# The last 128 tokens leave a dense expert product, and are summed from gathered rows

## The chip, the cores and the metric

The kernel runs on one core of a Trainium2 chip. The metric is the device time of one execution in microseconds (us); the time before is the median of three runs. The profile is of one further execution.

Engines are named as the profile names them: PE is TensorE (matmuls; PEld its weight loads), DVE is VectorE, ACT is ScalarE, POOL is GpSimd and SP is SyncE, which here only issues DMAs.

## What is computed

Two transformer blocks run one after the other on 512 tokens of width 1024, all in float32. The change touches only the last layer of the second block, an expert layer (PEER) with 128 x 128 = 16384 experts. An expert is one row of `u` and one row of `v`. Each token has 8 heads, and each head picks 16 experts, so a token sums 128 rows of `v`:

```python
def peer(hn, w_q, subkeys, u, v):
    q = (xt @ w_q).reshape(T, H, 2, PEER_QDIM // 2)
    s = jnp.einsum('thcd,cnd->thcn', q, subkeys)
    s1, i1 = lax.top_k(s[:, :, 0], K)             # K = 16, H = 8
    s2, i2 = lax.top_k(s[:, :, 1], K)
    cand = (s1[..., :, None] + s2[..., None, :]).reshape(T, H, K * K)
    sc, ci = lax.top_k(cand, K)
    idx = e1 * PEER_NKEYS + e2                    # e1, e2: entries of i1, i2 that ci names
    g = jax.nn.softmax(sc, axis=-1)
    a = jnp.einsum('cd,chkd->chk', xc, u[ic])     # ic: idx of these tokens
    act = gelu(a) * gc                            # gc: g of these tokens
    return jnp.einsum('chk,chkd->cd', act, v[ic])
```

## The kernel before

Activations lie transposed, feature on the partition and the 512 tokens along the free axis. The expert layer (`peer`) does not gather. It computes all 16384 activations of every token densely, multiplies them by a matrix G that is zero where a token did not pick the expert, and multiplies the result by all of `v`.

**Exact float32 by two halves.** A float32 operand is split into a high part in the faster format float32r and a low part, the rest. `mm3` (L317 to L322) makes a product of three matmuls: high by high, low by high, high by low. The weights are split on the way (`split`, L271): ACT copies the high part (`wh`), DVE subtracts (`wl`). `lin2` (L1096) loads one 512 KB weight tile (`raw`) with a DMA on SP, splits it and runs 8 x 3 matmuls of 512 columns into one PSUM bank (`acc1`). Three raw tiles and three split tiles are held.

**Routing** (`route`, `weights`, L1647 to L1740). For each block of 128 tokens DVE finds the 16 best of each key half and of the candidates, and leaves the experts' two numbers e1, e2 and the gates g, transposed by PE. `weights` builds G in DRAM, 16 tokens at a time: one-hot tiles on DVE and ACT, four matmuls of 256 columns for four tokens (L1734), and a store of 1 MB by POOL. There are 32 such time blocks, 512 matmuls.

**First product** (`up`, L1762). Unit e multiplies `u` by the activations, 24 matmuls, and applies gelu on ACT; SP stores the result GA[e] in DRAM. 128 units are needed. They are given out between the steps of routing by a running account of DVE's and ACT's estimated work (`PEER_NS`, `ROUTE_NS`), so that PE has matmuls while routing runs. 121 are done in that way, seven more in the first group of the second product.

**Second product** (L1781 to L1801). 16 groups of 8 units. POOL loads the group's slice of G (`gt`, 2 MB) and each unit's GA (`ga`, 256 KB); DVE multiplies them, ACT copies the high part and DVE subtracts (`hid`, 18 tiles: two for each of 8 units and one pair more). Then eight output tiles d follow, each a `lin2` over `v` with 24 matmuls of 512 columns, and DVE adds the bank into the residual X[d]. 16 x 8 x 24 = 3072 matmuls.

The tile framework sets the order of each engine's instructions from the written code and puts in the waits; an engine runs its own list in order.

A second form of matmul occurs early: `mod_group` (L467) multiplies a 128 x 32 float32 weight, and four such matmuls write to four groups of 32 output partitions:

```python
for k in range(8):
    j = 32 * (k % 4)
    nc.tensor.matmul(p[j:j + 32, 0:256], self.cs[:, k, :], ws[k], start=k < 4, stop=k >= 4, tile_position=(0, j))
```

Of the kernel before, what the change touches and what calls it, by code (L numbers as in the profile page):

```python
# [13 lines left out]
D, S, SC, T = 1024, 512, 256, 768  # L14
# [25 lines left out]
NGA = 6  # L40
# [31 lines left out]
TBW = 16  # L72
NTB = S // TBW
# [5 lines left out]
SHARE = 3  # L79
# [103 lines left out]
def pack2(i, o):  # L183
# [34 lines left out]
    o["pv"] = i["peer_v_2"].reshape(128, 16, 8, 8, 128).transpose(1, 3, 0, 2, 4)  # L218
    c, s = rope2_tables(np.arange(S))
# [11 lines left out]
    iota = np.tile(np.arange(128), (128, 1))  # L231
# [12 lines left out]
class K:  # L244
# [1357 lines left out]
    def peer(self, hs):  # L1602
# [14 lines left out]
        rt = fr.enter_context(self.tc.tile_pool(name="rt", bufs=1))  # L1617
        SCO = {}
# [13 lines left out]
        ET = [rt.tile([128, S], F32, name=n) for n in ("e1T", "e2T", "gT")]  # L1632
        GT = [rt.tile([128, S], F32R, name=n) for n in ("ghT", "glT")]
        U32 = mybir.dt.uint32
        CNT = [16 // (i + 1) for i in range(16)]
# [11 lines left out]
        def route(b):  # L1647
# [56 lines left out]
            p = self.acc1()  # L1704
            for j, src in enumerate((e12[:, 0], e12[:, 1], gz.rearrange("p h k -> p (h k)"))):
                nc.tensor.transpose(p[:, j * 128:j * 128 + 128], src, self.eye)
                nc.scalar.copy(ET[j][:, b * 128:b * 128 + 128], p[:, j * 128:j * 128 + 128])
            cs = slice(b * 128, b * 128 + 128)
            nc.scalar.copy(GT[0][:, cs], ET[2][:, cs])
            nc.vector.tensor_tensor(GT[1][:, cs], ET[2][:, cs], GT[0][:, cs], op=OP.subtract)  # L1710
# [31 lines left out]
        def routing():  # L1742

            for ns in route(0):
                yield ns, 0
            for b in range(4):
                r = route(b + 1) if b < 3 else iter(())
                due = 0.0
                for tb in range(NTB // 4 * b, NTB // 4 * (b + 1)):
                    for ns in weights(tb, SHARE if b == 3 else 0):  # L1750
                        yield ns
                        due += ROUTE_NS
                        while due > 0:
                            ns = next(r, None)
                            if ns is None:
                                break
                            due -= ns
                            yield ns, 0
                for ns in r:
                    yield ns, 0  # L1760

        def up(e, ahead):  # L1762
# [3 lines left out]
            if ahead:  # L1766
                GA[e] = dp.tile([128, S], F32, name=f"GA{e}")
                nc.sync.dma_start(out=GA[e], in_=ga)
            return ga

        GA = {}
        todo = [8 * g + e for g in list(range(2, 16, 2)) + list(range(1, 16, 2)) + [0] for e in range(8)]
        due = [0.0, 0.0]
        for ns in routing():
            due = [x + y for x, y in zip(due, ns)]
            while max(due) > PEER_NS and todo:
                due = [max(x - PEER_NS, 0.0) for x in due]
                up(todo.pop(0), True)
        fr.close()
        rb = self.es.enter_context(self.tc.tile_pool(name="rb", bufs=1))  # L1780
        for g in range(16):  # L1781
            gt = self.t("gt", [128, NTB, 8, TBW], bufs=2, pool=rb)
            nc.gpsimd.dma_start(out=gt.rearrange("p b e t -> p b (e t)"),
                                in_=G[:, :, 8 * g:8 * g + 8, :].rearrange("b p e t -> p b (e t)"))
            hid = []
            for e in range(8):
                if 8 * g + e in GA:
                    ga = self.t("ga", [128, S], bufs=NGA, pool=rg)
                    nc.gpsimd.dma_start(out=ga, in_=GA[8 * g + e])
                else:  # L1790
                    ga = up(8 * g + e, False)
                gv = ga.rearrange("p (b t) -> p b t", t=TBW)
                nc.vector.tensor_tensor(gv, gv, gt[:, :, e, :], op=OP.mult)
                hi = self.t("hid", [128, S], F32R, 18, rb)
                lo = self.t("hid", [128, S], F32R, 18, rb)
# [76 lines left out]
```

## Time and profile before

| what | value |
|---|---|
| median of 3 runs | 3765.06 us (3758.55 to 3765.51) |
| the profiled execution | 3763.02 us |
| its span, first to last instruction | 3761.3 us |
| granted TensorE clock, mean | 0.989 |
| PE busy | 3657.0 us, 97% |
| DVE / ACT / POOL busy | 2461.8 / 1749.6 / 159.2 us |
| moved by DMA | 490.28 MB |
| routing with units of the first product | 2360 to 3021 us |
| second product | 3060.5 to 3757.6 us |

The three runs lie within 0.2% of each other. A matmul's shown duration is its latency; matmuls overlap in the pipeline, and the distance between two starts is what one costs in a row. A line like L322 is that of a helper that serves the whole kernel, so the tile names tell which product a matmul belongs to: `hs` is the first product's input, `hid` the second's. A matmul of two float32 operands that are not float32r appears as two records.

### The profile page before, as it was taken

Reading aid. Unit: us, or ns where it says so; the run is one execution under the profiler, and the core shown is the slowest. Engines: PE = TensorE matmul, PEld = TensorE weight load, DVE = VectorE, ACT = ScalarE, POOL = GpSimd, SP = SyncE. Lnnn points to the kernel's source line nnn. Section 1 sums busy time; section 2 is a strip of 40 time slices with the busy share of each in tenths; the row PEclk is TensorE's granted clock in tenths of the full one; section 3 lists DMA queues with packets and bytes.
Section 4 is the critical chain, followed back from the end, with each engine's and each line's share of the span. In section 5 each row is a group of like instructions: output and inputs, shape, how many; then the busy total and the mean of one; then the engine's idle time right before and its main releaser. Section 6 shows DMA issues by size and latency. Waiting matters only on the chain.

```text
span 3761.3 us, 52800 instructions
## 1 busy us (share of the span) xinstructions
PE 3657.0 (97%) x19762; PEld 3004.0 (80%) x19762; DVE 2461.8 (65%) x4950; ACT 1749.6 (47%) x3452; POOL 159.2 (4%) x317
## 2 busy tenths in 40 slices
PE   8998999999999999999999999999999999999999
PEld 5866788888877878887778877878888888888887
DVE  5976644444788755564777669998766855555554
ACT  5267531111446732233566543777877733322232
POOL 0000000000000000000001000000000011111110
PEclk9999999999999999999999999999999999999999
DMA  6430432221341233334432333455555566666553
GB/s 210 132 107 13 123 118 63 67 63 62 106 144 56 74 118 95 95 96 137 117 98 83 100 98 115 155 171 177 184 179 171 199 212 200 201 196 192 189 185 115
DMA packets 155248, 490.28 MB, mean 130 GB/s; under 512 B 18368, under 2 KB 24832, under 8 KB 150768
## 3 DMA queue, kind: packets, MB, share of 16 engines
q1 hardware_dynamic: 128368, 374.48, 31.4%
q0 software_dynamic: 26624, 112.43, 8.8%
q8 instruction: 156, 2.56, 0.3%
q14 instruction: 100, 0.82, 0.1%
HBM read 408.86 MB, written 74.71 MB: 129 GB/s over the span
## 4 chain that ended last, share of the span: by engine, by line
PE 86%; DVE 8%; ACT 3%; DMA 2%; issue 1%; SPq 0%; ACTq 0%; POOL 0%; DVEq 0%; POOLq 0%
PE b L322 57%; PE a L322 19%; PE b L467 1%; DVE wl L277 1%; PE a L1734 1%; PE b L917 1%; PE b L568 1%; PE b L906 1%; PE b L1365 1%; PE a L1125 0%; DMA mraw<-in_wmod_dram 0%; DVE gst L1738 0%; PE b L1174 0%; ACT P L896 0%; DMA mg<-in_wmod_dram 0%
## 5 line engine op out<-in xcount | busy, mean ns | idle before, releaser
L276 ACT CAST wh<-raw 128x1024 fp32r<-128x1024 f32 (+2 forms) x531 | 547.3, 1031 | 1363.2 <-PE b L322 810.2
L322 PE MATMUL b<-hs,wh 128*128 128x512 f32 x2624 | 822.4, 394 | 4.4 <-ACT hs L1092 4.4
L277 DVE TENSOR_TENSOR wl<-raw,wh 128x1024 fp32r<-128x1024 f32 (+2 forms) x531 | 635.2, 1197 | 169.7 <-ACT wh L276 157.7
L322 PE MATMUL b<-hid,wh 128*128 128x512 f32 x2048 | 630.9, 389 | 0.0
L322 PEld LDWEIGHTS b<-hs,wh 128*128 128x128 f32 x2624 | 487.1, 190 | 107.3 <-ACT hs L1092 5.3
L322 PE MATMUL b<-hs,wl 128*128 128x512 f32 x1312 | 516.1, 393 | 0.9 <-DVE wl L277 0.9
L322 PEld LDWEIGHTS b<-hid,wh 128*128 128x128 f32 x2048 | 384.4, 188 | 80.6 <-DVE hid L1797 0.6
L322 PE MATMUL b<-hid,wl 128*128 128x512 f32 x1024 | 398.4, 389 | 0.0
L322 PE MATMUL b<-hh,wh 128*128 128x256 f32 (+1 forms) x1160 | 364.5, 351 | 3.7 <-DVE V L840 2.2
L322 PE MATMUL a<-hh,wh 128*128 128x512 f32 (+1 forms) x1144 | 354.6, 348 | 9.5 <-DVE y L1046 7.2
L322 PE MATMUL b<-hl,wh 128*128 128x256 f32 (+1 forms) x1160 | 356.0, 343 | 0.3 <-DVE hl L534 0.3
L322 PE MATMUL b<-hh,wl 128*128 128x256 f32 (+1 forms) x1160 | 355.0, 343 | 0.0
L322 PE MATMUL a<-hh,wl 128*128 128x512 f32 (+1 forms) x1144 | 349.8, 344 | 1.5 <-DVE wl L277 1.5
L322 PE MATMUL a<-hl,wh 128*128 128x512 f32 (+1 forms) x1144 | 350.5, 344 | 0.3 <-DVE hl L534 0.3
L322 PEld LDWEIGHTS b<-hs,wl 128*128 128x128 f32 x1312 | 248.2, 189 | 53.4 <-DVE wl L277 1.3
L322 PEld LDWEIGHTS b<-hh,wh 128*128 128x128 f32 x1160 | 200.3, 188 | 44.1 <-issue 4.8
L322 PEld LDWEIGHTS a<-hh,wh 128*128 128x128 f32 x1144 | 197.0, 188 | 44.6 <-issue 13.9
L322 PEld LDWEIGHTS b<-hl,wh 128*128 128x128 f32 x1160 | 200.7, 189 | 30.1 <-issue 1.2
L322 PEld LDWEIGHTS b<-hid,wl 128*128 128x128 f32 x1024 | 192.2, 188 | 39.6
L322 PEld LDWEIGHTS b<-hh,wl 128*128 128x128 f32 x1160 | 200.0, 188 | 27.9 <-issue 1.1
L322 PEld LDWEIGHTS a<-hl,wh 128*128 128x128 f32 x1144 | 197.2, 188 | 31.1 <-issue 2.9
L322 PEld LDWEIGHTS a<-hh,wl 128*128 128x128 f32 x1144 | 196.9, 188 | 30.6 <-DVE wl L277 2.3
(412 smaller groups left out, 5323.1 us busy)
## 6 DMA issues: line engine op xcount, KB each, us to landing
raw<-in_w_dram SPq DMA_DIRECT2D x134, 512.0 KB
raw<-in_pu_dram SPq DMA_DIRECT2D x128, 512.0 KB
raw<-in_pv_dram SPq DMA_DIRECT2D x128, 512.0 KB
raw<-in_win_dram SPq DMA_DIRECT2D x64, 512.0 KB
G<-gst POOLq DMA_DIRECT2D x32, 1024.0 KB, 4.9
gt<-G POOLq DMA_DIRECT2D x16, 2048.0 KB, 14.1
mraw<-in_wmod_dram SPq DMA_DIRECT2D x82, 384.0 KB
GA<-ga SPq DMA_DIRECT2D x121, 256.0 KB
```

The source lines that it names most:

```text
L276: nc.scalar.copy(hi, raw)
L277: nc.vector.tensor_tensor(lo, raw, hi, op=OP.subtract)
L322: nc.tensor.matmul(o, w[wi], xx[xi], start=start and xi == 0 and wi == 0, stop=stop and wi == 1)
L467: nc.tensor.matmul(p[j:j + 32, 0:256], self.cs[:, k, :], ws[k], start=k < 4, stop=k >= 4, tile_position=(0, j))
L568: nc.tensor.matmul(p[:, :w], self.ones[1024], s, start=k == 0, stop=k == 7)
L906: nc.tensor.transpose(p[:, j * 128:j * 128 + 128], Ps[e][:, kc * 128:kc * 128 + 128], self.eye)
L917: nc.tensor.matmul(o[pr, c % 2 * 128:c % 2 * 128 + 128], V[i][:, kc, pr], PT[e * nkb + kc], start=kc == 0, stop=kc == nkb - 1, tile_positi ...
L1365: nc.tensor.transpose(p[:, j * 128:j * 128 + 128], src, self.eye)
L1734: nc.tensor.matmul(p[:, i * 256:i * 256 + 256], A[:, i], W[:, i].rearrange("p j e -> p (j e)"), start=True, stop=True)
```

## The change

The first 384 tokens (`SG`) stay in the dense way; G has 24 time blocks of 16 tokens instead of 32, and the second product's matmuls have 384 columns. For the last 128 tokens:

- `route(3)` does not fill the tables for `weights`. It leaves two tiles of row numbers, `IV` (row of `v` of each pick and token, picks on the partition) and `IG` (place of the pick's activation in a DRAM array `GU`), and the gates `G3`.
- `up` stores the last 128 columns of each unit in `GU`; all 128 units now run before the second product, and none in it.
- Token t = 32 j + m belongs to column group j. For each m of 32, `rows(m)` fetches for four tokens their 128 rows of `v` (512 KB a token, by indirect DMA on POOL), `acts(m)` fetches their 128 activations (4 bytes each), multiplies them by the gates and puts them in column m of a 128 x 32 tile that is else zero (`az`). `sums(m)` runs eight fp32 matmuls into two banks `po`, that are held over all 32 sums.
- After the last unit, ACT copies `po` out, PE transposes it in eight pieces and DVE adds these to X.
- gt and ga loads move from POOL's queue to SP's; `ga` for the second product gets its own tiles `gd` (eight) in the pool `rb`, which takes the memory of the two pools given up after the first product.

```diff
-NTB = S // TBW
+SG = 384
+NTB = SG // TBW
+NVR = 8
...
-    def lin2(self, ap, hs, shape=(128, 8, 128)):
+    def lin2(self, ap, hs, shape=(128, 8, 128), n=S):
         w = self.wunit(ap, shape)
-        p = self.acc1()
+        p = self.acc1()[:, :n]
...
+            if last:
+                nc.vector.scalar_tensor_tensor(IV, dst[0], 128.0, dst[1], op0=OP.mult, op1=OP.add)
+                nc.vector.scalar_tensor_tensor(dst[0], dst[1], 128.0, dst[0], op0=OP.mult, op1=OP.add)
+                nc.vector.scalar_tensor_tensor(IG, dst[0], 128.0, iota, op0=OP.mult, op1=OP.add)
...
-        def up(e, ahead):
+        def up(e):
             p = self.lin2(a["pu"][e], hs)
-            ga = self.t("ga", [128, S], bufs=NGA, pool=rg)
+            ga = self.t("ga", [128, S], bufs=NGA, pool=ru)
             nc.scalar.activation(ga, p, AF.Gelu_apprx_tanh)
...
+            GA[e] = dp.tile([128, SG], F32, name=f"GA{e}")
+            nc.sync.dma_start(out=GA[e], in_=ga[:, :SG])
+            nc.sync.dma_start(out=GU[e], in_=ga[:, SG:])
...
+        for e in todo:
+            up(e)
         fr.close()
...
+        def rows(m):
+
+            for j in range(4):
+                v = VR[m, j] = self.t("vr", [128, D], bufs=NVR, pool=rb)
+                t = 32 * j + m
+                nc.gpsimd.indirect_dma_start(out=v, out_offset=None, in_=a["vn"],
+                                             in_offset=bass.IndirectOffsetOnAxis(ap=IV[:, t:t + 1], axis=0))
+
+        def acts(m):
+
+            c = self.t("ac", [128, 4], bufs=4, pool=rb)
+            for j in range(4):
+                t = 32 * j + m
+                nc.gpsimd.indirect_dma_start(out=c[:, j:j + 1], out_offset=None, in_=GU.rearrange("e p (t o) -> (e p t) o", o=1),
+                                             in_offset=bass.IndirectOffsetOnAxis(ap=IG[:, t:t + 1], axis=0))
+            nc.vector.tensor_tensor(c, c, G3[:, m::32], op=OP.mult)
+            z = VR[m] = self.t("az", [128, 4, 32], bufs=3, pool=rb)
+            nc.vector.tensor_tensor(z, c[:, :, None].to_broadcast([128, 4, 32]), hot[:, None, 31 - m:63 - m].to_broadcast([128, 4, 32]), op=OP.mult)
+
+        def sums(m):
+            z = VR.pop(m)
+            v = [VR.pop((m, j)) for j in range(4)]
+            for h in range(0, D, 512):
+                for j in range(4):
+                    nc.tensor.matmul(po[32 * j:32 * j + 32, h:h + 512], z[:, j, :], v[j][:, h:h + 512],
+                                     start=m == 0, stop=m == 31, tile_position=(0, 32 * j))
...
+            if g < 15:
+                load_gt(g + 1)
             for d in range(8):
-                p = self.lin2(a["pv"][g, d], hid)
-                nc.vector.tensor_tensor(X[d], X[d], p, op=OP.add)
+                if g < 15:
+                    load_ga(8 * g + 8 + d)
+                p = self.lin2(a["pv"][g, d], hid, n=SG)
+                nc.vector.tensor_tensor(X[d][:, :SG], X[d][:, :SG], p, op=OP.add)
+                m, r = divmod(8 * g + d, 4)
+                if r == 1 and m < 31:
+                    acts(m + 1)
+                if r == 2:
+                    sums(m)
+                    if m < 30:
+                        rows(m + 2)
+        y = self.t("vr", [128, D], bufs=NVR, pool=rb)
+        nc.scalar.copy(y, po)
```

On PE, between two units of the second product, before; a unit's 24 matmuls end and the next unit's begin at once (`b` is the accumulator, `hid` the split activations, `wh` and `wl` the split weights):

```order
L322 MATMUL b_29053<-hid_28973,wl_29050 128x512
L322 MATMUL b_29053<-hid_29011,wh_29049 128x512
L322 MATMUL b_29053<-hid_29012,wh_29049 128x512
L322 MATMUL b_29053<-hid_29011,wl_29050 128x512
L322 MATMUL b_29085<-hid_28745,wh_29081 128x512
L322 MATMUL b_29085<-hid_28746,wh_29081 128x512
```

The same place now, after the third unit of the first group:

```order
L325 MATMUL b_28614<-hid_28524,wh_28610 128x384
L325 MATMUL b_28614<-hid_28525,wh_28610 128x384
L325 MATMUL b_28614<-hid_28524,wl_28611 128x384
L1823 MATMUL a_28479<-vr_28463,az_28486 32x512
L1823 MATMUL a_28479<-vr_28465,az_28486 32x512
L1823 MATMUL a_28479<-vr_28467,az_28486 32x512
L1823 MATMUL a_28479<-vr_28469,az_28486 32x512
L1823 MATMUL a_28479<-vr_28463,az_28486 32x512
L1823 MATMUL a_28479<-vr_28465,az_28486 32x512
L1823 MATMUL a_28479<-vr_28467,az_28486 32x512
L1823 MATMUL a_28479<-vr_28469,az_28486 32x512
L325 MATMUL b_28664<-hid_28489,wh_28660 128x384
```

Eight matmuls of the sums stand between units, once in four units, and a unit's matmuls are narrower.

On POOL, at the end of routing before: the loads for the second product follow the last store of G directly, while PE's list has the 168 matmuls of seven units between the last routing matmul and the first on `hid`:

```order
L1740 DMA G<-gst_28407 128x2048
L1789 DMA ga_28742<-GA_28704 128x512
L1740 DMA G<-gst_28586 128x2048
L1783 DMA gt_28740<-G 128x32x128
L1783 DMA gt_29271<-G 128x32x128
L1789 DMA ga_29273<-GA_24465 128x512
```

The same loads now, on SP, at the end of the first product:

```order
L1782 DMA GA_28398<-ga_28396 128x384
L1783 DMA GU<-ga_28396 128x128
L285 DMA raw_28692<-in_pv_dram 128x1024
L1782 DMA GA_28434<-ga_28432 128x384
L1783 DMA GU<-ga_28432 128x128
L285 DMA raw_28726<-in_pv_dram 128x1024
L1828 DMA gt_28445<-G 128x24x128
L1833 DMA gd_28447<-GA_20741 128x384
```

The loads of gt and gd moved behind the two stores of the last unit of the first product; weight tiles for the first six units of the second product stand ahead of them. PE's list has 600 matmuls, 25 units, between the last routing matmul and the first on `hid`.

On POOL in the middle of the second product before, the loads of one group:

```order
L1783 DMA gt_30213<-G 128x32x128
L1789 DMA ga_29936<-GA_25303 128x512
L1789 DMA ga_29943<-GA_25359 128x512
L1789 DMA ga_29950<-GA_25423 128x512
L1789 DMA ga_30215<-GA_21234 128x512
```

And now, the gathers for one sum, of activations (`ac`) and of rows (`vr`):

```order
L1812 DMA ac_29844<-GU,ig 128x1 x4
L1804 DMA vr_29010<-in_vn_dram,iv 128x1024
L1804 DMA vr_29012<-in_vn_dram,iv 128x1024
L1804 DMA vr_29014<-in_vn_dram,iv 128x1024
L1804 DMA vr_29016<-in_vn_dram,iv 128x1024
```

POOL has eight indirect DMAs for each sum in place of nine plain ones for each group of eight units.

## Rows read from the trace of the kernel before

**Rows 1.** The page: busy times and the chain that ended last

```profile
PE 3657.0 (97%) x19762; PEld 3004.0 (80%) x19762; DVE 2461.8 (65%) x4950; ACT 1749.6 (47%) x3452; POOL 159.2 (4%) x317
...
PE 86%; DVE 8%; ACT 3%; DMA 2%; issue 1%; SPq 0%; ACTq 0%; POOL 0%; DVEq 0%; POOLq 0%
PE b L322 57%; PE a L322 19%; PE b L467 1%; DVE wl L277 1%; PE a L1734 1%; PE b L917 1%; PE b L568 1%; PE b L906 1%; PE b L1365 1%; PE a L1125 0%; DMA mraw<-in_wmod_dram 0%; DVE gst L1738 0%; PE b L1174 0%; ACT P L896 0%; DMA mg<-in_wmod_dram 0%
```

**Rows 2.** Stretches: us; busy PE, PEld, DVE, ACT, POOL; clock; DMA share; GB/s

```profile
2360.00:3021.00 661.00, 655.90 (x3100) 546.65 (x3099) 533.69 (x1147) 505.01 (x1274) 16.55 (x31) 1.00 0.53 179
3021.00:3060.50 39.50, 38.62 (x173) 31.68 (x172) 18.48 (x22) 15.05 (x23) 6.69 (x8) 1.00 0.81 252
3060.50:3757.60 697.10, 697.02 (x3074) 576.38 (x3072) 380.09 (x497) 203.41 (x249) 86.27 (x130) 1.00 0.58 182
3757.60:3761.30 3.70, 0.00 (x0) 0.00 (x0) 0.65 (x1) 0.00 (x0) 0.00 (x0) 0.93 0.19 71
```

**Rows 3.** Groups of PE in the second product: busy us, mean ns, idle before

```profile
L322 PE MATMUL b<-hid,wh 128*128 128x512 f32 x2048 | 630.9, 389 | 0.0
L322 PE MATMUL b<-hid,wl 128*128 128x512 f32 x1024 | 398.4, 389 | 0.0
```

**Rows 4.** Timeline of PE, 384-column matmuls: start us, us, instruction

```profile
2051.67 0.33 PE L322 MATMUL a<-hi,qhi 128*128 128x384 f32 x1
...
2053.41 0.33 PE L322 MATMUL a<-hi,qlo 128*128 128x384 f32 x1
```

**Rows 5.** Groups of DVE in the second product

```profile
L1793 DVE TENSOR_TENSOR ga<-ga,gt 128x512 f32<-128x512 f32 x121 | 79.0, 685 | 105.9 <-DMA ga<-GA 105.9
L1797 DVE TENSOR_TENSOR hid<-ga,hid 128x512 fp32r<-128x512 f32 x122 | 77.3, 684 | 1.4 <-ACT hid L1796 1.4
```

**Rows 6.** Routing's matmuls: their group, and the timeline at the first

```profile
L1734 PE MATMUL a<-ohW,ohA 128*128 128x256 f32 x512 | 80.8, 287 | 10.5 <-ACT ohW L1730 10.2 <-DVE gst L1738 0.3
...
2351.08 1.46 PE L1734 MATMUL a<-ohW,ohA 128*128 128x256 f32 x4 [5.42 <-ACT ohW L1730]
```

**Rows 7.** fp32 matmuls: timelines of mod_group and of L1174, and their groups

```profile
100.13 1.07 PE L467 MATMUL b<-mraw,cs 128*32 128x256 f32 x16
101.13 0.50 PE L322 MATMUL a<-hh,wh 128*128 128x512 f32 x1
...
L467 PE MATMUL b<-mraw,cs 128*32 128x256 f32 x656 | 55.1, 393 | 3.0 <-DMA mraw<-in_wmod_dram 3.0
...
1798.15 1.02 PE L1174 MATMUL b<-sq,c 128*128 128x512 f32 x2
...
L1174 PE MATMUL b<-sq,c 128*128 128x512 f32 x36 | 18.6, 598 | 0.0
```

**Rows 8.** Groups of ACT from 2360 to 3060 us: gelu, and the high part

```profile
L1765 ACT ACTIVATE ga<-b 128x512 f32<-128x512 f32 x114 | 67.2, 590 | 0.3 <-PE b L322 0.3
L1796 ACT CAST hid<-ga 128x512 fp32r<-128x512 f32 x7 | 4.3, 622 | 12.8 <-issue 6.7 <-DVE ga L1793 6.1
```

**Rows 9.** SP's issues of the outputs: duration ns min/median/max, first and last

```profile
L1852 SPq DMA_DIRECT2D out_dram<-x x8: 332/338/344, 3720.2 to 3758.3; - x8
```

**Rows 10.** From issue to landing: all DMAs of GA, and gt's loads

```profile
DMA to landing us min/median/max: 3.0/4.9/14.5
...
gt<-G POOLq DMA_DIRECT2D x14, 2048.0 KB, 14.1
```

**Rows 11.** Stretches, as in rows 2: after routing's first wait, and the fullest DMA

```profile
2347.70:2354.40 6.70, 3.32 (x9) 2.89 (x10) 6.70 (x23) 4.94 (x16) 0.00 (x0) 0.50 0.36 117
...
20.00:30.00 10.00, 7.72 (x63) 2.63 (x62) 7.55 (x17) 6.32 (x11) 0.00 (x0) 0.83 1.03 407
```

**Rows 12.** Groups of POOL in the second product

```profile
L1789 POOL DMA_DIRECT2D ga<-GA x116 | 62.5, 539 | 542.3 <-DVE hid L1797 535.9 <-issue 2.4
L1783 POOL DMA_DIRECT2D gt<-G x14 | 23.8, 1703 | 24.9 <-DVE ga L1793 24.9
```

**Rows 13.** DMA queue of POOL in the second product: packets, MB, share of 16 engines

```profile
q0 software_dynamic: 16694, 59.83, 26.9%
```

More of the change, by code (lines that the diff above doesn't have):

```diff
@@ L218, in pack2 @@
     o["pv"] = i["peer_v_2"].reshape(128, 16, 8, 8, 128).transpose(1, 3, 0, 2, 4)
+    o["vn"] = i["peer_v_2"]
     c, s = rope2_tables(np.arange(S))
@@ L1704, in route @@
             p = self.acc1()
+            last = b * 128 >= SG
+            dst = [self.t("e3", [128, 128], bufs=2, pool=rt) for _ in range(2)] + [G3] if last else [e[:, b * 128:b * 128 + 128] for e in ET]
             for j, src in enumerate((e12[:, 0], e12[:, 1], gz.rearrange("p h k -> p (h k)"))):
                 nc.tensor.transpose(p[:, j * 128:j * 128 + 128], src, self.eye)
[L1707 to L1710, printed above, removed]
+                nc.scalar.copy(dst[j], p[:, j * 128:j * 128 + 128])
+            if last:
+                nc.vector.scalar_tensor_tensor(IV, dst[0], 128.0, dst[1], op0=OP.mult, op1=OP.add)
+                nc.vector.scalar_tensor_tensor(dst[0], dst[1], 128.0, dst[0], op0=OP.mult, op1=OP.add)
+                nc.vector.scalar_tensor_tensor(IG, dst[0], 128.0, iota, op0=OP.mult, op1=OP.add)
+            else:
+                cs = slice(b * 128, b * 128 + 128)
+                nc.scalar.copy(GT[0][:, cs], ET[2][:, cs])
+                nc.vector.tensor_tensor(GT[1][:, cs], ET[2][:, cs], GT[0][:, cs], op=OP.subtract)
             yield 0
@@ L1745, in routing @@
                 yield ns, 0
-            for b in range(4):
-                r = route(b + 1) if b < 3 else iter(())
+            for b in range(3):
+                r = route(b + 1)
                 due = 0.0
-                for tb in range(NTB // 4 * b, NTB // 4 * (b + 1)):
-                    for ns in weights(tb, SHARE if b == 3 else 0):
+                for tb in range(NTB // 3 * b, NTB // 3 * (b + 1)):
+                    for ns in weights(tb, SHARE if b == 2 else 0):
                         yield ns
@@ L1760, in routing @@
                     yield ns, 0
-        def up(e, ahead):
+        def up(e):
             p = self.lin2(a["pu"][e], hs)
-            ga = self.t("ga", [128, S], bufs=NGA, pool=rg)
+            ga = self.t("ga", [128, S], bufs=NGA, pool=ru)
             nc.scalar.activation(ga, p, AF.Gelu_apprx_tanh)
[L1766 to L1769, printed above, removed]
+            GA[e] = dp.tile([128, SG], F32, name=f"GA{e}")
+            nc.sync.dma_start(out=GA[e], in_=ga[:, :SG])
+            nc.sync.dma_start(out=GU[e], in_=ga[:, SG:])
         GA = {}
-        todo = [8 * g + e for g in list(range(2, 16, 2)) + list(range(1, 16, 2)) + [0] for e in range(8)]
+        todo = list(range(128))
         due = [0.0, 0.0]
@@ L1781, in peer, with load_ga @@
+        def load_ga(e):
+            gas[e] = self.t("gd", [128, SG], bufs=8, pool=rb)
+            nc.sync.dma_start(out=gas[e], in_=GA[e])
+        hot = rb.tile([128, 64], F32, name="hot")
+        nc.gpsimd.memset(hot, 0.0)
+        nc.gpsimd.memset(hot[:, 31:32], 1.0)
+        load_gt(0)
+        for e in range(8):
+            load_ga(e)
+        for m in range(2):
+            rows(m)
+        po = self.acc()
+        acts(0)
         for g in range(16):
-            gt = self.t("gt", [128, NTB, 8, TBW], bufs=2, pool=rb)
@@ L1783, in peer @@
-            nc.gpsimd.dma_start(out=gt.rearrange("p b e t -> p b (e t)"),
-                                in_=G[:, :, 8 * g:8 * g + 8, :].rearrange("b p e t -> p b (e t)"))
+            gt = gts.pop(g)
             hid = []
             for e in range(8):
[L1787 to L1791, printed above, removed]
+                ga = gas.pop(8 * g + e)
```

27 lines of the change are left out of this document (22 added, 5 removed).

## The prediction

> **What bounds the kernel now.** I read the busy times first, then the chain of waits, then a table of stretches, then the groups of instructions of the last stretch, and only after that the queues. TensorE is busy for 97% of the span, and the chain that ended last lies on it for 86%, 57% in matmuls into the one-bank accumulators [rows 1]. The table of stretches says where: from 2360 us on PE never rests, and the stretch from 3060.5 to 3757.6 us, the second product of the experts, is 697.1 us with 697.02 us of PE busy [rows 2]. In it stand 3072 matmuls of 512 columns (2048 + 1024) with no idle time before them [rows 3]. So one costs 697.1 / 3072 = 0.227 us; its shown mean of 0.389 us is latency. Other engines have room there: DVE 380 us, ACT 203 us, POOL 86 us, and the DMA engines are at 0.58 at 182 GB/s [rows 2]. Time comes off the span where PE gets less to do, as long as nothing with room now runs out of it.
>
> **The dense product.** It keeps its 3072 matmuls but each has 384 columns. The trace has eleven such matmuls back to back, from 2051.67 to 2053.41 us: ten steps of 0.174 us [rows 4]. 3072 x 0.174 = 534.5 us, so **-162.6 us**. DVE's and ACT's share of that work shrinks with it: their 512-wide groups [rows 5] become 384 wide.
>
> **The routing weights.** A quarter of the 512 matmuls on L1734 goes, 128. A quarter of their 80.8 us [rows 6] is 20, but that counts tails that lie over the next matmul; at half a 512-column matmul's 0.227 it is 15. I take **-16 us**. The DVE and ACT work that goes with them lay under PE and gives nothing more. The first wait of this stage, 5.42 us for ACT [rows 6], comes before any of the removed blocks and stays.
>
> **The new sums.** 32 times eight fp32 matmuls of 512 columns, each using 32 columns of the array, in four column groups. mod_group has the same form with 256 columns: its eight matmuls are 16 records and take 1.00 us from the first start to the next instruction's [rows 7]; one record lasts 0.393 us on average, so one after the other without overlap they would take over 3 us. Four run at once: four sets at (1.07 - 0.39) / 3 = 0.22 us. Of the two records of a 512-column fp32 matmul the second starts 1.02 - 0.60 = 0.42 us after the first (L1174: the pair's extent less one duration) [rows 7]; with the rounding I take 0.43, so 0.86 for a whole one. So one sum is 4 x 0.43 = 1.72 us, and changing the array's form costs what the 1.00 us has over 4 x 0.22, some 0.12 us, and about as much on the way in. 32 x 1.95 = **+62 us**; bounds 55 (no change of form) and 220 (no overlap: 256 x 0.86).
> The Trainium skill (TensorEngine Tiling, Key Properties) says that a change of tiling mode drains the array; the trace agrees, with the 0.12 us. Its page TensorE: Matmul & The Clock Gate (Measured speedup vs the span model) gives 2.38x for three column tiles; four at that efficiency would be 3.2x, and the sums would be an estimated 75 us instead of 62. The rows above show nearer to four, so I stay at 62.
>
> **The stage boundary.** Before, the first G tile is read by POOL as soon as routing ends, and seven expert units of the first product still run on PE meanwhile; PE is busy 38.62 of 39.5 us there [rows 2]. Now all 128 units come first and 25 of them follow the last routing matmul, but the first gt load stands on SP's queue behind the stores of the last unit, and its buffers are those of a pool that must be given up, so it waits for these stores too. Nothing on PE covers this chain: gelu 0.59 [rows 8]; two store issues at 0.33 [rows 9] and a landing of at least 3.0 us (median 4.9, which includes reads), I take 3.5 [rows 10]; the gt load, 14.1 us for 2 MB [rows 10], three quarters of which is 10.6, lengthened because eight row gathers of 512 KB start with it, so 13 (at most double, 21); the first gd behind it, 1; multiply and cast at three quarters of 0.685 and 0.62 [rows 5, 8], 1. That is 20 us. Then the first unit goes at DVE's pace: eight experts at two operations of 0.51 us are 8.2 us against PE's 4.2, so 4 more. After an idle 5.42 us the granted clock was 0.50 for 6.7 us, the 1.2 GHz level [rows 6, 11]; most of that falls into DVE's pace, 1 more. **+25 us**, bounds 16 and 38.
>
> **The end.** Now only the last of the eight outputs is late: from the last matmul to the end 3.7 us [rows 2]. After, all eight wait for the 128-column additions, behind a copy (which a last dense unit hides) and eight transposes: about 1 us of PE, then eight issues at 0.338 us [rows 9] and 2.1 MB to write at 314 to 395 GB/s (below), 5.3 to 6.7 us. **+7 us** in all, bounds 3 and 10.
>
> **Queues, and what hides.** POOL loses ga and gt loads (0.54 and 1.70 us each [rows 12]) and gets 256 indirect DMAs. No row shows an indirect one. With those two as bounds they are 138 to 436 us of POOL in a stage of 534.5 + 62 = 596, so hidden; they bind from 596 / 256 = 2.3 us each. A sum's rows are asked for two sums (37 us) ahead, and a POOL wait there holds up only later gathers. SP gets gt and gd loads between its weight loads, so a late gd holds up raw tiles behind it, and DVE, which already waits 105.9 us for ga [rows 5], waits for gd in front of wl. Three weight tiles split ahead are 12.5 us of cover instead of 16.3.
> The DMA engines: weights 67.1 MB, rows 67.1, gd 25.2, gt 25.2, together 184.6 MB. At the stage's own rate per share, 182 / 0.58 = 314 GB/s, that is 588 us; at the fullest stretch of the trace, 407 GB/s at 1.03 [rows 11], so 395, it is 467 us. Added to this are 16384 gathered single elements, 1024 an engine. Their price is between nothing and a whole packet's: q0's 16694 packets took 26.9% of 16 engines over 697 us [rows 13], 0.18 us, so 0 to 184 us in all. I take 0.06 us, 61 us, since four bytes move but a packet has a fixed part; this is the softest number here. Sum: 528 to 649 us against PE's 596 + 25. So DMA nearly fills the stage without setting its length, and bursts will cost PE something: **+12 us**, bounds 0 and 50.
>
> **Sum.** -162.6 - 16 + 62 + 25 + 7 + 12 = -72.6. The profiled execution took 3763.0 us (span 3761.3), so 3690.4; the median of the runs is 2.0 higher, so the forecast is **3692 us**.
>
> **Rivals.** (a) *The DMA engines set the stage.* For it: 588 + 61 = 649 us above. Against: 407 GB/s was reached. The stage takes 649 + 25 instead of 596 + 12 + 25: 3733 us. From 0.09 us an element (681 - 588 = 93 us over 1024) the whole gain is gone. The Trainium skill (DMA: Bandwidth & Descriptors, Specifications) says that a transfer under 512 B makes the engine read, modify and write, which speaks against these element gathers; it states no price, and no run here shows one. (b) *POOL sets the stage, slower than before.* If one indirect DMA takes POOL 3 us, 256 are 768 us: 768 - 596 - 12 = +160, 3852 us. It turns slower from (608 + 73) / 256 = 2.66 us. For it: the indices must be read from SBUF and 128 addresses built. Against: 4096 pieces of 512 B took only 1.70 us [rows 12]. (c) *The column groups don't run at once* with 512 columns and four different right-hand tiles: 220 us for 62, 3850 us. Against: the four at once in [rows 7]. (d) *Almost no bubble and no stalls:* bubble 16, bursts 0, end 3: 3692 - 9 - 12 - 4 = 3667 us, with shorter sums (55) 3660.
>
> **How the numbers follow.** Forecast 0.62 (own range 3670 to 3720), (d) 0.09, (a) 0.18, (b) 0.08, (c) 0.03. A difference of 0.2%, 7.5 us, is about what a measurement tells from no change. Of (a) I give 0.11 to faster, 0.04 to within, 0.03 to slower. Faster: 0.62 + 0.09 + 0.11 = 0.82; same 0.04; slower 0.03 + 0.08 + 0.03 = 0.14. The range 3655 to 3750 leaves out (b), (c), the upper third of (a) and a little below (d): 0.19.
>
> **What would show it.** Right: matmuls from hid at 0.174 us, the 512 records of the sums in sets of four at 0.43 us; one PE gap of about 20 us before the first hid matmul, its releaser gt or gd; a stage of 600 to 625 us after it. Wrong: PE idle all through the stage behind raw, gd or vr loads at a DMA share near 1 (a); POOL busy throughout, with sums waiting for vr or ac (b); records of the sums strung out singly (c). My sum also falls if the fp32 sums break up the stream of weight loads at more than 0.2 us a time, or if idle gaps at group boundaries lower the granted clock again and again.

## The result and the profile after

The changed kernel takes 3702.6 us (median of 3701.4 to 3707.1) against 3764.0 for the kernel before beside it: ratio 0.984, 95% interval 0.983 to 0.986. The profiled execution of it is its slowest, 3707.1 us with a span of 3705.3, so the traces differ by 56.0 us where the medians differ by 61.4. The stage that does the sums and the dense product is the last but one row here, to be laid against [rows 2].

The page of the changed kernel, then its stretches (us; busy PE, PEld, DVE, ACT, POOL; clock; DMA share; GB/s): first product with routing, gap, second product, end.

```profile
PE 3561.1 (96%) x20154; PEld 2972.7 (80%) x20154; DVE 2351.8 (63%) x4926; ACT 1649.6 (45%) x3172; POOL 344.8 (9%) x430
...
DMA packets 245780, 536.03 MB, mean 145 GB/s; under 512 B 26656, under 2 KB 131424, under 8 KB 242320
```

```profile
2356.70:3048.80 692.10, 686.95 (x3177) 570.76 (x3177) 482.79 (x1100) 435.97 (x1033) 12.77 (x24) 1.00 0.50 169
3048.80:3071.30 22.50, 0.07 (x2) 0.01 (x1) 1.78 (x2) 1.92 (x3) 13.07 (x16) 0.59 0.89 312
3071.30:3696.70 625.40, 613.97 (x3587) 556.60 (x3588) 343.58 (x572) 194.19 (x253) 269.29 (x243) 0.99 0.82 281
3696.70:3705.30 8.60, 0.81 (x8) 0.57 (x6) 2.11 (x9) 0.00 (x0) 0.00 (x0) 0.78 0.66 244
```

Groups of PE and POOL from 3071.3 us on (busy us, mean ns, idle time before and its releaser); the first two answer to [rows 3], the last two to nothing in the kernel before.

```profile
L325 PE MATMUL b<-hid,wh 128*128 128x384 f32 x2048 | 534.1, 342 | 24.8 <-DMA gd<-GA 22.4 <-DVE hid L1855 2.4
L325 PE MATMUL b<-hid,wl 128*128 128x384 f32 x1024 | 348.7, 340 | 9.0 <-DVE wl L280 9.0
L1823 PE MATMUL a<-vr,az 128*32 128x512 f32 x512 | 61.6, 598 | 0.0
...
L1804 POOL DMA_INDIRECT vr<-in_vn_dram,iv x120 | 146.7, 1222 | 282.0 <-PE a L1823 244.0 <-issue 25.0 <-PE b L325 13.0
L1812 POOL DMA_INDIRECT ac<-GU,ig x123 | 123.1, 1001 | 40.0 <-issue 33.1 <-DMA vr<-in_vn_dram,iv 3.3 <-DVE x L1863 2.4
```

The dense matmuls, which had no idle time before them, now have 33.8 us: 22.4 in the one gap ahead of the stage and 11.4 spread over it. The sums wait for nothing. POOL spends 1.2 us on each gather of rows and 1.0 on each gather of elements, and waits for PE itself.

One sum in PE's timeline (start us, us, instruction):

```profile
3209.31 0.34 PE L325 MATMUL b<-hid,wl 128*128 128x384 f32 x1
3209.58 1.92 PE L1823 MATMUL a<-vr,az 128*32 128x512 f32 x16
3211.43 0.62 PE L325 MATMUL b<-hid,wh 128*128 128x384 f32 x2
3211.89 0.34 PE L325 MATMUL b<-hid,wl 128*128 128x384 f32 x1
```

A sum is 1.85 us from its first start to the next matmul's, and the matmuls at its two sides are 0.20 us further apart than elsewhere: from 3209.31 to 3211.89 are 2.58 us, three dense ones at 0.176 are 0.53, so one sum costs 2.05.

**Where the 56.0 us come from.** First product with routing -17.5; gap +22.4; stage 625.3 for 696.8, that is -71.5; end 8.7 for 3.8, +4.9; and +5.7 in code ahead of the first routing matmul that the change doesn't touch (by chance: that matmul starts at 2351.1 us before and at 2356.8 here, and anywhere from 2348.5 to 2356.7 in the traces of the experiments). Within the stage the sums take 32 x 1.854 = 59.3 us and the dense product 566.0, where 3072 x 0.174 would be 534.5. So some 31 us of the forecast's gain are missing there, and the experiments are about them. I split them by the distances between the starts of neighbouring dense matmuls: those over 0.3 us hold 18.2 us beyond 0.174 each ("gaps" below; more than the idle time shown, as matmuls at a granted clock of 0.50, 0.32 us apart, count), the two sides of the sums 32 x 0.20 = 6.4, and all the others stand at 0.1760 instead of 0.174, 6 us.

What a gap looks like in the changed kernel: ACT, which makes the high half of a weight tile, then DVE, then the row of PE that waited.

```profile
3102.33 1.05 ACT L279 CAST wh<-raw 128x1024 fp32r<-128x1024 f32 x1 [3.17 <-PE b L325]
```

```profile
3109.65 0.17 DVE L1814 TENSOR_TENSOR ac<-ac,g 128x4 f32<-128x4 f32 x1 [9.79 <-DMA ac<-GU,ig]
3109.73 1.22 DVE L280 TENSOR_TENSOR wl<-raw,wh 128x1024 fp32r<-128x1024 f32 x1
3110.87 0.16 DVE L1814 TENSOR_TENSOR ac<-ac,g 128x4 f32<-128x4 f32 x1
3110.94 0.55 DVE L1863 TENSOR_TENSOR x<-x,b 128x384 f32<-128x384 f32 x1
3115.02 0.22 DVE L1814 TENSOR_TENSOR ac<-ac,g 128x4 f32<-128x4 f32 x1 [3.53 <-DMA ac<-GU,ig]
```

```profile
3111.01 0.69 PE L325 MATMUL b<-hid,wl 128*128 128x384 f32 x1 [1.91 <-DVE wl L280]
```

DVE stands 9.79 us before four fetched columns. The low half of a weight tile, whose high half ACT had made by 3103.4, is next on DVE and starts at 3109.73; PE runs dry for 1.91 us behind it. And since a raw weight tile is given back only when its low half is made, SP's next weight load is late too.

Not every gap hangs on ac. Of the 18.2 us, 3.6 lie in the stage's first 10 us (DVE's pace and a granted clock of 0.50), 5.2 come right behind a wait of DVE for ac, and 9.4 behind a low half that DVE made only after a wait of 5.3 to 6.3 us for gd. The first of these gd loads had itself been issued late, behind the second wait for ac above; for the other three the trace leads to no wait for ac. One of them:

```profile
3513.95 0.56 DVE L1851 TENSOR_TENSOR gd<-gd,gt 128x384 f32<-128x384 f32 x1 [5.58 <-DMA gd<-GA]
3514.43 1.22 DVE L280 TENSOR_TENSOR wl<-raw,wh 128x1024 fp32r<-128x1024 f32 x1
```

```profile
3515.70 0.44 PE L325 MATMUL b<-hid,wl 128*128 128x384 f32 x1 [1.60 <-DVE wl L280]
```

### The profile page after: what moved, and what is told of

It reads as the page before. It is cut to its first block, busy times and chain, and to the rows that moved or that the text cites. A ratio compares the mean times of both kernels' runs of the same rounds, so it can differ in the third digit from the quotient of the medians.

```text
span 3705.3 us, 53755 instructions
## 1 busy us (share of the span) xinstructions
PE 3561.1 (96%) x20154; PEld 2972.7 (80%) x20154; DVE 2351.8 (63%) x4926; ACT 1649.6 (45%) x3172; POOL 344.8 (9%) x430
## 4 chain that ended last, share of the span: by engine, by line
PE 84%; DVE 8%; DMA 3%; ACT 3%; issue 1%; SPq 0%; POOL 0%; ACTq 0%; DVEq 0%
PE b L325 54%; PE a L325 19%; PE a L1823 2%; DVE wl L280 2%; PE b L470 1%; PE b L920 1%; DMA gd<-GA 1%; PE b L571 1%; PE a L1749 1%; PE b L909 1%; PE b L1368 1%; DMA mraw<-in_wmod_dram 1%; DVE gst L1753 1%; PE a L1128 0%; PE b L1177 0%
## 5 line engine op out<-in xcount | busy, mean ns | idle before, releaser
L325 PE MATMUL b<-hid,wh 128*128 128x384 f32 x2048 | 534.1, 342 | 24.8 <-DMA gd<-GA 22.4
L325 PEld LDWEIGHTS b<-hid,wh 128*128 128x128 f32 x2048 | 373.5, 189 | 53.5 <-ACT hid L1854 22.9
L325 PE MATMUL b<-hid,wl 128*128 128x384 f32 x1024 | 348.7, 340 | 9.0 <-DVE wl L280 9.0
```

The lines of the kernel that those rows point to most:

```text
L325: nc.tensor.matmul(o, w[wi], xx[xi], start=start and xi == 0 and wi == 0, stop=stop and wi == 1)
```

## The experiments

The theories: *order* (DVE stands in order before data of DMAs, weight tiles behind it), *traffic* (the DMA engines bring too much), *queue* (gt and gd loads ahead of weight loads on SP's queue), *form or place* (the matmuls themselves are slower). All times are in us; stage and gaps are from the profiled execution, "ac", "gd" and "raw" are the waits of DVE and ACT for these DMAs from 3077 to 3600 us. "Gaps" here also has what a sum waited or was stretched: 4.3 us in e12, 5.8 in e9, 0.5 in e3.

| kernel | median | ratio to before | stage | gaps | ac | gd | raw |
|---|---|---|---|---|---|---|---|
| changed kernel | 3702.6 | 0.984 | 625.3 | 18.2 | 37.4 | 70.9 | 124.2 |
| e1_rows_once | 3690.9 | 0.981 | 617.9 | 11.4 | 44.0 | 9.0 | none |
| e2_no_elements | 3691.0 | 0.981 | 614.7 | 7.7 | none | 70.1 | 141.2 |
| e3_loads_pool | 3720.7 | 0.990 | 650.3 | 42.1 | 139.4 | 61.1 | 66.6 |
| e4_dense_alone | 3610.2 | 0.961 | 542.4 | 7.9 | none | 10.1 | none |
| e6_cover | 3689.9 | 0.980 | 631.0 | 31.0 | 41.3 | 68.8 | 121.5 |
| e7_hid_moved | 3706.0 | 0.984 | 628.9 | 28.9 | 40.2 | 76.7 | 144.7 |
| e8_loads_act | 3747.1 | 0.994 | 665.6 | 56.4 | 42.8 | 42.4 | none |
| e9_gt_in_parts | 3709.9 | 0.986 | 624.2 | 17.1 | 70.0 | 50.2 | 81.6 |
| e10_all | 3736.6 | 0.993 | 674.2 | 70.9 | 129.6 | 6.4 | 45.5 |
| e11_scale_pool | 3687.4 | 0.979 | 610.6 | 4.1 | on POOL | 45.2 | 41.5 |
| e12_cover_scale_pool | 3664.0 | 0.974 | 606.5 | 6.5 | on POOL | 56.0 | 79.4 |

The ratios have 95% intervals of about +-0.0015 to +-0.002. For 69 us of ACT's waits in e9 and 58 in e10 the trace names no releaser, so their "raw" can be too low. e5 has one run, and stands in its own section.

### Taking traffic away: e1, e2, e4

```diff
             for j in range(4):
-                v = VR[m, j] = self.t("vr", [128, D], bufs=NVR, pool=rb)
+                if m > 1:
+                    VR[m, j] = VR[m % 2, 4 + j]
+                    continue
+                v = VR[m, j] = VR[m, 4 + j] = self.t("vr", [128, D], bufs=NVR, pool=rb)
```

> Leaves out the row gathers of the third sum and of all later ones: the eight tiles of the first two sums are read again, 61 MB less by DMA, the last 128 tokens' values are not the reference's. Everything else stays, the element gathers too. The dense matmuls of the second product now take 566 us where 3072 x 0.174 = 534.5 were forecast, 32 too many. Theory traffic (the row gathers fill the DMA engines, so weight tiles land late): the DMA share of that stretch falls from 0.80 to about 0.45, the idle gaps of PE go, the stage falls by 20 to 30 us, total about 3677. Theory queue (loads of gt and gd stand ahead of weight tiles on SP's queue): the loads stay where they are, at most 8 us less, total 3695 to 3703. Theory form (384-column matmuls between fp32 sums simply cost 0.183 on average): nothing changes, 3702 +- 4.

```diff
+            nc.gpsimd.memset(c, 1.0)
-            for j in range(4):
+            for j in range(0):
                 t = 32 * j + m
                 nc.gpsimd.indirect_dma_start(out=c[:, j:j + 1], ...
```

> Leaves out the gathers of single elements (the activations of the last 128 tokens are replaced by ones; those tokens' values are not the reference's). Theory price (the prediction's 0.06 us of DMA engine an element): 16384 elements over 16 engines free 61 us of each, the DMA share of the stage falls from 0.80 to 0.70 and the time by some 10 us. Theory free element (a packet of 15 ns each that lies between others): share unchanged within 0.03. Theory order (DVE stands in order before ac, 37 us of its waits): DVE's wait for ac goes and with it some of wl's lateness, 3 to 8 us less, total 3695 to 3700. Theories traffic and form: 3702 +- 4.

e4 leaves out rows(), acts(), sums() and their calls.

> Leaves out the last 128 tokens' whole second product: no row gathers, no element gathers, no sums (zeros are added). What stays of the stage is the dense product of 384 tokens with its loads. Forecast by the prediction's term: 3072 x 0.174 = 534.5 us. Theory traffic: dense part 535 to 542, as the DMA share falls to about 0.5; total 3702 - 59 - 25 = 3618. Theory queue: gt and gd still stand ahead of weight tiles, 550 or more, total 3630. Theory form (384 columns cost 0.183 here whatever stands beside): 560 to 566, total about 3643.

The stretch from 3077 to 3600 us of the changed kernel, of e1 and of e2 (columns as above):

```profile
3077.00:3600.00 523.00, 512.64 (x3004) 464.86 (x3004) 293.78 (x499) 164.32 (x215) 248.00 (x226) 0.99 0.86 297
```

```profile
3077.00:3600.00 523.00, 519.40 (x3064) 473.29 (x3066) 306.07 (x499) 167.17 (x215) 116.82 (x115) 1.00 0.63 194
```

```profile
3077.00:3600.00 523.00, 521.21 (x3083) 474.06 (x3085) 297.95 (x493) 167.65 (x216) 129.11 (x133) 1.00 0.87 304
```

Without rows (share 0.63) or without elements (share 0.87) the stage loses 7.4 and 10.6 us, gaps mostly. The gaps behind the stage's first 10 us are 14.6 us in the changed kernel, 5.2 in e1 and 2.0 in e2. So it is not traffic alone: e2 carries as much as the changed kernel and has fewer gaps. Nor is it DVE's standing alone: e1 waits for ac for 44 us and pays 5.2, with no weight tile late. e1's total lies between the forecasts of *traffic* (3677) and *queue* (3695 or more); e2's 3691.0 is the 10 us less or so of the theory *price*, but the share didn't fall to the 0.70 that goes with it; it is 4 below the forecast of *order*. Elements cost the DMA engines nothing that the share shows. e4 has the dense part at 542.1 us, 8 above the forecast's 534.5, about what its gaps hold. Its total, 3610.2, is 8 below the forecast of *traffic*: its matmuls stand closer, at 0.1734 us (next section), and its gap ahead of the stage is 14.5 us for 22.4.

### The matmuls themselves: e5, e7

```diff
-            for h in range(0, D, 512):
-                for j in range(4):
+            for j in range(4):
+                for h in range(0, D, 512):
```

> The sums' two loops change places: first the two 512-column matmuls of one column group, then those of the next. The changed kernel's sum takes 1.854 us and its records stand in four sets of four, 0.43 apart. Theory of the prediction (the four groups run at once only because neighbours in PE's order sit in different groups): each group's pair now runs one after the other, at 2 x 0.86 a group, some 6 to 7 us a sum, 32 x 5 = +160 us, total about 3860. Rival (the array holds four groups' work whatever the order): 1.85 us a sum, 3703.

One run: 3705.7 us, and a sum from its first start to the next matmul's is 1.87 us:

```profile
3208.10 1.94 PE L1823 MATMUL a<-vr,az 128*32 128x512 f32 x16
3209.98 0.62 PE L325 MATMUL b<-hid,wh 128*128 128x384 f32 x2
```

The 16 records again start in four sets of four, 0.43 to 0.45 apart. The rival was right: groups that are not neighbours in PE's program still run at once. How the array does this isn't shown.

```diff
-            c = self.t("ac", [128, 4], bufs=4, pool=rb)
+            c = self.t("ac", [128, 32], bufs=4, pool=rb)[:, 0:4]
```

> Only a place in SBUF changes: the four ac buffers get 128 B each instead of 16 B, so everything allocated behind them, the hid tiles too, lies 448 B higher, at the same remainder of 512 B as in the kernel with the dense product alone. Undisturbed 384-column matmuls follow each other at 0.1760 us in the changed kernel from its first unit on, in a pattern of five, and at 0.1734 in the dense product alone. Theory place (the tiles' address costs the 2.6 ns): 0.1734 again, 3072 x 2.6 ns = 8 us less, total about 3695. Theory sums (whatever stands in PE's stream beside them): 0.1760, 3702 +- 4.

Dense matmuls behind each other in e7, the first and the last of 21 steps:

```profile
3426.07 0.34 PE L325 MATMUL b<-hid,wl 128*128 128x384 f32 x1
...
3429.72 0.33 PE L325 MATMUL b<-hid,wl 128*128 128x384 f32 x1
```

And in the changed kernel, the first and the last of 33 steps:

```profile
3424.71 0.34 PE L325 MATMUL b<-hid,wl 128*128 128x384 f32 x1
...
3430.52 0.34 PE L325 MATMUL b<-hid,wl 128*128 128x384 f32 x1
```

3.65 us for 21 steps are 0.1738 each, and 5.81 for 33 are 0.1761; over the whole stage the undisturbed ones are 0.1734 apart, against 0.1760. So the place in SBUF was worth 2.6 ns a matmul, 8 us in all, as *place* said; which tile's place it is, of all that moved, isn't shown. The time, forecast at 3695, is the same as without it nevertheless: PE, 8 us quicker, ran into 10.7 us more of gaps. This suggests that what feeds PE, and not PE, sets the pace of the stage here.

### Other queues for gt and gd: e3, e8, e9

```diff
-            nc.sync.dma_start(out=gas[e], in_=GA[e])
+            nc.gpsimd.dma_start(out=gas[e], in_=GA[e])
```

and the same for gt; in e8 nc.scalar in place of nc.gpsimd; in e9 on SP, but gt in eight parts of three blocks, one ahead of each load_ga.

> The loads of gt and gd are issued by POOL on its own queue, as before the change, and no longer by SP between the weight tiles. Theory queue: weight tiles are no longer behind them, the waits of ACT for raw (124 us) fall by half or more, the dense part comes down by 15 to 25 us, total about 3683. Theory traffic: the same bytes move, 3702 +- 5. Against a gain speaks that gd now stands on POOL behind row gathers that wait for a sum on PE (244 us of POOL waits): if that decides, DVE waits longer for gd and the total is 3710 or more. The first loads also stand ahead of the row gathers, so the gap before the stage stays at 20 to 24 us.

> The loads of gt and gd are issued by ACT on a hardware queue of its own, neither between SP's weight tiles nor behind POOL's row gathers. Theory queue in its pure form (weight tiles are late because gt and gd stand ahead of them on SP's queue): ACT's waits for raw fall from 124 us to under 50, the idle gaps of PE (18 us over 0.3 us each) go, total 3685 to 3692. Theory traffic (without the row gathers the waits for raw were gone and the gaps 11 us, though gt and gd stood where they stand): the waits stay within a third of 124 us, total 3702 +- 6. ACT's own issues cost it about 0.3 us each, 144 in 625 us, which has room.

> The load of gt (3072 pieces of 512 B a group of experts) is issued in eight parts, one ahead of each gd load, in place of one at the group's start; the same bytes on the same queue. In the changed kernel SP's issue of the next weight tile behind a whole gt lasts 2.2 to 7.1 us in 12 of the groups, 0.33 us everywhere else. Theory block (a queue full of gt's pieces holds up the weight tiles): no issue of a weight tile over 1 us, ACT's waits for raw fall from 124 us to under 60, the gaps of PE over 0.3 us fall from 18 us to under 11, total about 3693. Theory traffic (rows, weights and gt together are what makes a tile late, in whatever pieces): the long issues go, the waits for raw stay over 80 us, total 3702 +- 4.

None brought a gain. e3's total lies in its third case (3710 or more), but through another wait than that case named: on POOL the gd loads and the gathers stand behind one another, DVE's wait for ac, and not for gd, grows from 37 to 139 us, and the stage by 25. The totals of e8 and e9 lie outside all their forecasts. On ACT the weight tiles are never late, as *queue* said, but eight issues fall between ACT's casts of hid at each group's boundary, so that DVE's hid, and PE behind it, come late. ACT's timeline, and PE's group from 3077 to 3600 us:

```profile
3245.67 0.33 ACTq L1833 DMA_DIRECT2D gd<-GA  x1
3246.12 0.51 ACT L1854 CAST hid<-gd 128x384 fp32r<-128x384 f32 x1
3246.20 0.33 ACTq L1833 DMA_DIRECT2D gd<-GA  x1
```

```profile
L325 PE MATMUL b<-hid,wh 128*128 128x384 f32 x1593 | 427.3, 347 | 29.3 <-DVE hid L1855 29.3
```

In e9 the issues behind gt still take up to 4.7 us (one of gt's parts or the weight load after it), and the median is no better than the changed kernel's. One of its sums is stretched to 7.7 us by waits for which the trace names no releaser.

### Covering the gap: e6, e10

e6 opens the second product's pool once routing ends and makes the first eight experts' tiles among the last four units of the first product:

```diff
-        ru = fr.enter_context(self.tc.tile_pool(name="ru", bufs=1))
+        ru = self.es.enter_context(self.tc.tile_pool(name="ru", bufs=1))
...
-        po = self.acc()
-        acts(0)
+        for e in todo[:-4]:
+            up(e)
+        tail = todo[-4:]
         for g in range(16):
...
             for e in range(8):
+                if g == 0 and e % (8 // 4) == 0:
+                    up(tail.pop(0))
...
+            if g == 0:
+                po = self.acc()
+                acts(0)
```

> The second product's pool is opened as soon as routing ends (the gelu buffers stay, the routing buffers go), so its first gt, gd and rows are loaded under the last 25 units of the first product, and the first eight experts are weighted and split among the last four of these. Prediction's theory of the gap (22.4 us of stores, gt load, gd load and the first multiply with nothing on PE): it goes but for a few us, and with it the low clock at the start of the stage (3 us); the total falls by 18 to 26 us, about 3680. Rival (only moved: the first sums then wait for ac, or the first units for weight tiles that stand behind those loads): at most 10 us less, 3693 or more.

The gap went to nothing, but the time fell by 12.7 us only, between the two forecasts and nearer the rival's: the gaps grew by 12.8, and some 20 of their 31 us lie in the stage's first 60. Not all of the 12.7 is the cover's. With its pool elsewhere in SBUF, e6 has its undisturbed dense matmuls at 0.1734 us, as e7 has, which is worth 8 us; so have e10 and e12. A wait of DVE there, and from 3050 to 3110 us the group of PE behind it:

```profile
3094.62 0.21 DVE L1813 TENSOR_TENSOR ac<-ac,g 128x4 f32<-128x4 f32 x1 [9.84 <-DMA ac<-GU,ig]
```

```profile
L325 PE MATMUL b<-hid,wl 128*128 128x384 f32 x68 | 24.8, 365 | 10.4 <-DVE wl L280 10.4
```

e10 adds gt in parts, sums two units later and the elements' fetch behind the rows' of the same sum, further ahead of its use.

> Three edits together: the cover of the gap as in e6_cover; gt in eight parts as in e9_gt_in_parts; the elements for a sum fetched seven units before DVE touches them, and all sums two units later (the last at unit 126 as before), so that DVE no longer stands before ac with weight tiles behind it. In e6_cover the gap had gone, but 31 us of gaps of over 0.3 us stood in the stage, 19 of them in its first 60 us, where DVE stood five times behind ac (ac waited for the last units' stores). Theory that these waits are the rest of the loss: gaps under 10 us in all, stage 600 to 608, total 3658 to 3668, faster than both kernels. Rival (the stage is held by the DMA engines at 300 GB/s, and what is taken off one wait turns up at another): stage 620 or more, total 3680 or more.

A plain miss, 34 us slower than the changed kernel; the total and the stage lie where the rival put them (3680 or more, 620 or more), at 251 GB/s and not at its 300. DVE's wait for ac rose to 130 us and stood at the groups' boundaries, where the hid tiles are due (idle before PE there: 31 us behind DVE's hid). The theory's mechanism showed, with the sign turned: I had moved the fetch behind the row gathers on POOL, and in DVE's order the multiply that uses it stands between the first and the second of the next group's hid tiles, so that the others wait with it:

```profile
3234.01 0.55 DVE L1864 TENSOR_TENSOR hid<-gd,hid 128x384 fp32r<-128x384 f32 x1
3237.86 0.17 DVE L1817 TENSOR_TENSOR ac<-ac,g 128x4 f32<-128x4 f32 x1 [3.29 <-DMA ac<-GU,ig]
3237.96 1.97 DVE L1864 TENSOR_TENSOR hid<-gd,hid 128x384 fp32r<-128x384 f32 x4
```

### The test of order: e11, e12

```diff
-            nc.vector.tensor_tensor(c, c, G3[:, m::32], op=OP.mult)
+            nc.gpsimd.tensor_tensor(c, c, G3[:, m::32], op=OP.mult)
...
-            nc.vector.tensor_tensor(z, c[:, :, None]...
+            nc.gpsimd.tensor_tensor(z, c[:, :, None]...
```

> The two short operations that turn the fetched elements into the sums' stationary tiles go from DVE to POOL; the gathers and all else stay. So DVE no longer stands before ac (37 us of its waits in the changed kernel, 13 times), and no low half of a weight tile waits behind it. Theory order (the loss that went when the elements were left out, 10.6 us of the stage, was DVE's standing): the gaps of PE over 0.3 us fall from 18 us to about 8, total 3690 to 3695. Rival (what went there was the 16384 elements' own claim on POOL, whose row gathers then come sooner, and on the DMA engines): no change, 3702 +- 4. Against both: POOL now stands before ac itself, some 5 us for each of 32 sums, on top of 282 us of gathers in 625; if a sum then waits for its rows, 3710 or more.

> The cover of e6_cover with the two short operations on POOL as in e11_scale_pool. In e6_cover 19 us of gaps stood in the first 60 us of the stage, where DVE stood five times behind ac while ac's gathers waited for the last units' stores. Theory order: these gaps go but for the first sum's own wait, and the later ones as in e11_scale_pool: stage about 610, total 3668 to 3676. Rival (the gap's cover is given back in whatever form, since the stage is held by what the DMA engines bring): 3685 to 3692, as e6_cover.

The same stretch in e11, and in e12 the first product with routing, the stage and the end:

```profile
3077.00:3600.00 523.00, 523.00 (x3095) 475.77 (x3094) 299.93 (x440) 168.36 (x216) 275.78 (x290) 1.00 0.89 304
```

```profile
2354.00:3049.60 695.60, 687.73 (x3177) 570.64 (x3178) 495.77 (x1126) 439.86 (x1040) 20.97 (x34) 1.00 0.56 188
3049.70:3656.10 606.40, 600.81 (x3587) 544.95 (x3586) 331.20 (x483) 193.42 (x247) 305.82 (x312) 1.00 0.82 279
3656.10:3665.30 9.20, 0.91 (x9) 0.68 (x7) 2.13 (x9) 0.00 (x0) 0.00 (x0) 0.78 0.61 229
```

This settles it. All bytes and queues are as in the changed kernel, and the DMA engines are even fuller (0.89), yet PE is busy for all of the 523 us; the gaps are 4.1 us, all in the stage's first 10 us, and ACT's waits for weight tiles fell by two thirds. POOL now stands before ac for 113 us, where nothing hurries. The gain is somewhat larger than forecast, 15 us. The gaps behind gd went too, with DVE's waits for gd down from 70.9 to 45.2 us.

Another reading is that POOL, held by its own wait, asks for rows later, and that this and not DVE's order freed the weight tiles. From 3077 to 3600 us POOL's waits for the sums on PE, before it can fetch rows, are 204 us in the changed kernel, 72 in e11 and 357 in e2. The gaps go both where POOL is held and where it is freer, so its pace is not the cause; what the two have in common is that DVE no longer waits for ac.

With the gap covered as well the kernel takes 3664.0 us, ratio 0.974 (0.972 to 0.975), faster than both and 4 below its forecast. The cover is not all that e12 adds: its undisturbed dense matmuls are 0.1734 us apart, as in e7, so some 8 of the 38.6 us that it gains on the changed kernel are the place's. A stretch of 15 steps, and then the first sum, whose wait for its tile makes the largest distance left, 4.5 us:

```profile
3063.05 0.33 PE L325 MATMUL b<-hid,wl 128*128 128x384 f32 x1
...
3065.65 0.34 PE L325 MATMUL b<-hid,wl 128*128 128x384 f32 x1
3070.20 2.33 PE L1822 MATMUL a<-vr,az 128*32 128x512 f32 x12 [4.21 <-POOL az L1815]
```

Two gaps of 1.1 and 0.6 us behind waits of DVE for gd remain.

The Trainium skill (Perfetto Trace Analysis, Tensor Engine Instruction) says that ACT, DVE and GpSimd are strict FIFO. The runs agree: in the 9.79 us above, a weight tile whose high half was made stood ready for DVE for the last 6 us.

## Why the prediction was right

The measured median, 3702.6 us, is 10.6 above the forecast of 3692, and the mechanism, a lighter dense product less the sums, a gap and some stalls, is what the traces show. Its terms against the profiled execution:

- **Dense product**, -162.6. The 0.174 was read from another place in the kernel [rows 4]; here the undisturbed matmuls stand at 0.176, which e7 showed to be the tiles' place in SBUF. Mis-sized by 6.
- **Routing weights**, -16: -17.5.
- **Sums**, +62: 59.3 and 6.4 at their two sides, 65.7. The four groups run at once with sets at 0.43 us, as read from [rows 7]; a sum costs 2.05 for 1.95, since from the last set to the next dense matmul are 0.52 and the two sides add 0.20.
- **Stage boundary**, 20 of wait: 22.4, in the chain as told (stores, gt, gd). SP's first gd issue stood 4.3 us behind gt, which the forecast had not counted. The 4 + 1 us of DVE's pace and clock came to 3.6, the gaps of the stage's first 10 us.
- **Bursts and stalls**, 12: the rest of the gaps, 14.6. That the size fits is luck, since the 12 was chosen between bounds of 0 and 50 and not worked out, and the reason was only half right: the text put it down to DMA engines that nearly fill the stage. e11 fills them more and has none of the 14.6. The sentence that named the cause in passing was that DVE "waits for gd in front of wl"; it missed that ac would join it, and e11 that took ac away cured both.
- **End**, +7: +4.9.

These make 6 + 3.7 + 2.4 - 1.4 + 2.6 - 1.5 - 2.1 = 9.7; with the 5.7 of chance that is the difference of the traces, 16.7 (3707.1 for 3690.4), but for a microsecond.

The rivals: (a) stood on 0.06 us of DMA engine for each gathered element. e2 took all 16384 away and the share went from 0.86 to 0.87, not down by 0.1: the price is near nothing, and the Trainium skill's rule on transfers under 512 B (DMA: Bandwidth & Descriptors, Specifications) is borne out by no cost that these runs show. (b) POOL takes 1.0 and 1.2 us a gather, 270 us in the stage, far from the 2.66 each that the rival needed. (c) fell with the sets of four. (d) had the gap and the stalls too small, though e12 shows that they need not be there.

## What to carry to other kernels

Before giving an engine a short operation that waits for a DMA, look at what stands behind it in that engine's order: here two operations of 0.2 and 0.3 us on DVE cost some 15 us in all, and an engine with slack took them at no cost that shows. A gap that has been covered, or matmuls that have been made quicker, give time only when the next thing is not late already; so cure the waits within the stage first. When a loss vanishes on leaving out work, ask whether it was the work's load or its wait: move the wait alone to tell.

## What the runs showed of the hardware

- Matmuls of 384 columns in a row took 0.1734 us each in e7 and 0.1760 in the changed kernel, from which it differs only by tiles that lie 448 B higher in SBUF; in the slower place one in five takes 0.182.
- Four column groups worked at once in fp32 whether PE's program went round the groups or group by group (1.85 us a sum in the changed kernel, 1.87 in e5).
- In the changed kernel the issue of a weight load on SP behind a load of 3072 pieces of 512 B lasted 2.2 to 7.1 us in 12 groups of 14, where the usual one lasts 0.33; in the other two it took 0.33 and 1.5.
- Gathers of 128 single elements cost POOL 1.0 us, nearly as much as gathers of 128 rows of 4 KB (1.2 us), and the DMA engines nothing that could be seen.
